# A hand-written TensorE order in the last block of a three-block kernel, with the scan's step sizes computed early

## The chip, the core and the metric

One core of a Trainium2 chip runs the whole program. The metric is the device time of one execution in microseconds (us); smaller is better. The engines are PE (TensorE), DVE (VectorE), ACT (ScalarE), POOL (GpSimd) and SP (SyncE, which issues most DMAs here). Everything is computed in 32 bits: a matrix product is made of three PE passes over a high and a low part.

## What is computed

Three blocks over 1024 tokens of 1024 features. The first is an attention with a window and a state-space mixer, the second an attention on the best 256 keys. The third, which the change is mostly about, is:

```python
h = layer_norm(x, ln_emb_g, ln_emb_b)
xs, z, bm, cm, dt_raw, glu, cgate = jnp.split(h @ w_in, SPLITS, axis=-1)
xbc = silu(causal_depthwise_conv(concat([xs, bm, cm]), ssm_conv_w, ssm_conv_b))   # 4 taps
dt = softplus(dt_raw + dt_bias)                        # step sizes
y = ssd_chunked(xh, dt, -exp(a_log), bm, cm)           # scan over 8 chunks of 128 tokens
y_ssm = group_rms((y + d_skip * xh) * silu(z)) * ssm_norm_g
u = causal_depthwise_conv(glu[..., :D] * sigmoid(glu[..., D:]), conf_conv_w, conf_conv_b)   # 31 taps
y_conf = silu(layer_norm(u, conf_ln_g, conf_ln_b)) * silu(cgate)
out = concat([y_ssm, y_conf]) @ w_out + b_out
h = layer_norm(ALPHA * h + out, ln1_g, ln1_b)
h = layer_norm(ALPHA * h + sigmoid(h @ w_ple_gate) * (p @ w_ple_proj), ln2_g, ln2_b)
```

## The kernel before, in words

A planner that simulates the program orders the instructions of every engine and chooses when a tile gets memory. It goes by the order of the trace (the order in which the Python code emits instructions), lets what is ready run first, and takes a priority: `high_priority(offset=...)` moves an instruction ahead, as for the weight loads in `wpiece` (L104). On the chip each engine runs its instructions in the order that the planner wrote.

`phase_c` (L1239) is the third block. First come the two halves of glu (L1263), with `c_vectors` (L1452) behind the first product: it loads vectors as rows and turns them with PE into columns (`cw` for the 31-tap convolution, its norm and glu's bias; `sw` for the 4-tap convolution). `xbc` (L1527) makes the raw step sizes and the 4-tap convolutions; the first tap is a DVE instruction (L1552), the other three too (L1554). The 31-tap convolution runs on DVE (L1289), 31 instructions for each of 8 tiles. `conf_norm` (L1490) takes the mean (`mu`, PE), subtracts it (L1503, DVE), squares (ACT), adds up (POOL), makes the variance (`var`, PE) and its root, spreads it (`rb`, PE), multiplies (L1523, DVE) and applies Silu (L1524).

`ssd` (L1568) begins with the step sizes: a chain of some 26 small DVE instructions on `spt`, three products (`acs`, `atot`, `acsT`), and the cumulative sums written to memory (`d_cs`). Then eight chunks follow. A chunk loads its decays as broadcast rows (`ld`, L1636), adds (L1637) and takes Exp, masks with `cb` (L1645, L1650), makes three products on POOL (`xd`, `xe`, `xh`), and for each of two groups runs `yoff`, `ydiag` (eight heads), and `inc`, which moves the state `st` on.

Beside this, PE has products that need nothing of the scan: the gate `cgate` (L1304), `z` (L1319), and the half of the output product that takes `cc` (L1348); the latter needs cc normalised and gated on POOL (L1314), and split into two parts in `msC` (L1336, L1337). They are traced after `ssd`, and the planner puts them where PE is free. Its PSUM has two banks for these, one for transposes, three (`sd`) for norm and scan, two for the convolution. Behind the block the second half of the output product (`prep`, L1368), the norm and the last gate follow.

In the second block, `DSA` (L1126) runs units of a query block and a key group: its bias loads are `lgB` (L1165), and the weights `wo` of the first half of that block's output product are loaded ahead of all units (L983).

Of the kernel before, what the change touches and what calls it, by code (L numbers as in the profile page):

```python
# [56 lines left out]
class K:  # L57
# [94 lines left out]
    def form1(self, out, hnT, tok0, wt, nk, w, wc0=0, start=True, stop=True):  # L152

        for k in range(nk):
            self.mm3(out, hnT[:, 0, k, tok0:tok0 + P], hnT[:, 1, k, tok0:tok0 + P],
                     wt[k][:, 0, wc0:wc0 + w], wt[k][:, 1, wc0:wc0 + w],
                     start and k == 0, stop and k == nk - 1)

# [676 lines left out]
def phase_b(k, x, hout, hB):  # L835
# [145 lines left out]
    with ExitStack() as c2:  # L981
        dp = c2.enter_context(k.pool("b_dsa"))
        wo = k.wchunk(Wo, 0, 512)  # L983
        ds = DSA(k, ep, dp, d_q, d_T, d_gate, kT, vB, sc, kg, mix)
        units = [(b, kv) for b in DORD for kv in range(2)]
        pipeline(ds, units, lambda b: out_tile(k, mo, gp, b, 0, [mix], wo, x, hout, "sq", 1))
# [6 lines left out]
    hnC = hp.tile([P, 2, KT, L], F32R, name="hnTC")  # L993
    gb = op.tile([P, D], F32, name="gbC")
# [131 lines left out]
class DSA:  # L1126
# [22 lines left out]
    def front(self, b, kv):  # L1149
# [10 lines left out]
        for i in range(4):  # L1160
# [3 lines left out]
            with k.tc.high_priority(offset=WPRIO):  # L1164
                nc.sync.dma_start(lg[:, :n], dap(self.d_T, h * P * 1152 + 127 + P * (7 - b), [[1151, P], [1, n]]))  # L1165
# [73 lines left out]
def phase_c(k, out, hC):  # L1239
# [8 lines left out]
    cw = vp.tile([P, 8, 36], F32, name="cw")  # L1248
# [6 lines left out]
    def stage():  # L1255
        return stg.tile([P, 512], F32, tag="s", name="stg", bufs=3)
# [21 lines left out]
    with ExitStack() as cx:  # L1278
        xbc(k, cx.enter_context(k.pool("c_xbc")), W, hnT, sw, dtt, d_xs, d_bc)
# [13 lines left out]
    conf_norm(k, up, cc, acc, cw)  # L1293
    sV.close()

    sS, (sp,) = stack(k.pool("ssd"))
    ssd(k, sp, dtt, dtx, d_xs, d_bc, d_ys, d_cs)

    for ch in range(2):
        w = k.wchunk(W, 4624 + ch * 512, 512)  # L1300
        for m in range(4):
            for th in range(2):
                ps = k.mm()
                k.form2(ps, hnT, th * 512, w, KT, m * P)  # L1304
                gt = stage()
                S.activation(gt, ps, AF.Silu)
                r0 = (ch * 4 + m) * P
                nc.scalar.dma_start(d_cg[r0:r0 + P, th * 512:th * 512 + 512], gt)
    for ct in range(8):
        for th in range(2):  # L1310
            cs = slice(th * 512, th * 512 + 512)
            cg = stg.tile([P, 512], F32, tag="cg", name="cgl", bufs=2)
            nc.sync.dma_start(cg, d_cg[ct * P:(ct + 1) * P, cs])
            G.tensor_tensor(cc[:, ct, cs], cc[:, ct, cs], cg, op=ALU.mult)  # L1314
    for ch in range(2):
        w = k.wchunk(W, 1024 + ch * 512, 512)
        for tt in range(NT):
            ps = k.mm()
            k.form1(ps, hnT, tt * P, w, KT, 512)  # L1319
            zt = stage()  # L1320
            S.activation(zt, ps, AF.Silu)
            nc.scalar.dma_start(d_z[tt * P:(tt + 1) * P, ch * 512:ch * 512 + 512], zt)
    sR.close()
    k.wdve = WDVE[4]

    with ExitStack() as co:
        op = co.enter_context(k.pool("c_o", side="right"))
        bo = op.tile([P, D], F32, name="bo")
        k.bcast_row(bo, ins["b_out_2"][0], D)
        w = [[k.wpiece(Wo, kk + 8, [(ch * 512, 512)], pool=op if ch * 8 + kk >= 13 else None, nx=3)  # L1330
              for kk in range(8)] for ch in range(2)]
        held = []
        for tt in range(NT):
# [6 lines left out]
            V.scalar_tensor_tensor(r, r, ALPHA, bo, op0=ALU.mult, op1=ALU.add)  # L1340
            held.append((tt, m, r))
            if tt == NT - 2:
                continue
            for ch in range(2):
                cs = slice(ch * 512, ch * 512 + 512)
                for t_, m, r in held:
                    ps = k.mm()
                    k.form1(ps, m, 0, w[ch], 8, 512)  # L1348
                    V.tensor_tensor(r[:, cs], ps, r[:, cs], op=ALU.add)
                    nc.sync.dma_start(d_r[t_ * P:(t_ + 1) * P, cs], r[:, cs])  # L1350
            held = []
    sS.close()
    sF.close()

# [4 lines left out]
    with ExitStack() as co:  # L1359
# [4 lines left out]
        k.bcast_row(bb, ins["ln1_b_2"][0], D)  # L1364
        w = [[k.wpiece(Wo, kk, [(ch * 512, 512)], scale=sng[:, kk:kk + 1], pool=op if ch * 8 + kk >= 13 else None, nx=3)
              for kk in range(8)] for ch in range(2)]

        def prep(tt):  # L1368
# [18 lines left out]
            r = op.tile([P, D], F32, tag="r", name="rS", bufs=2)  # L1387
            nc.sync.dma_start(r, d_r[ts_, :])
            return m, r
# [19 lines left out]
        for tt in range(NT):  # L1409
            pt = op.tile([P, 256], F32, tag="pt", name="pt", bufs=2)  # L1410
# [41 lines left out]
def c_vectors(k, p, cw, sw, dtx, sng):  # L1452
# [6 lines left out]
    rows = p.tile([36, D], F32, tag="u", name="rows", bufs=2)  # L1459
    with k.tc.high_priority(offset=2 * WPRIO):  # L1460
        nc.sync.dma_start(rows[0:31], ins["conf_conv_w_2"][0])
    for i, n in enumerate(("conf_conv_b_2", "conf_ln_g_2", "conf_ln_b_2")):
        with k.tc.high_priority(offset=2 * WPRIO):
            nc.sync.dma_start(rows[31 + i:32 + i], ins[n])
    with k.tc.high_priority(offset=2 * WPRIO):
        nc.sync.dma_start(rows[34:36], ins["b_glu_2"][0].rearrange("(a b) -> a b", a=2))
    for h in range(2):
        ps = k.tp()
        for i in range(4):
            T.transpose(ps[:, i * 36:(i + 1) * 36], rows[:, (h * 4 + i) * P:(h * 4 + i + 1) * P], k.ident[:36, :36])  # L1470
        V.tensor_copy(cw[:, h * 4:h * 4 + 4].rearrange("p a b -> p (a b)"), ps[:, :144])
# [18 lines left out]
def conf_norm(k, p, cc, acc, cw):  # L1490
# [5 lines left out]
    for th in range(2):  # L1496
        ps = k.ps("sd", "mu")
        T.matmul(ps, on, acc[:, th * 512:th * 512 + 512], start=True, stop=True)
        mu.append(ps)
    for ct in range(8):  # L1500
# [11 lines left out]
    for tt in range(NT):  # L1512
        T.matmul(ps[:, tt * 2:tt * 2 + 2], acc[:, tt * P:(tt + 1) * P], on[:, 0:2], start=True, stop=True)
    V.tensor_scalar(rs[:, 0], ps[:, :16].rearrange("p (a b) -> p a b", b=2)[:, :, 0], 1e-5, None, op0=ALU.add)
    k.rstd(rs[:, 1], rs[:, 0], 8)
    rb = [k.ps("sd", "rb0"), k.ps("sd", "rb1")]
    for tt in range(NT):
        T.matmul(rb[tt // 4][:, (tt % 4) * P:(tt % 4 + 1) * P], rs[:, 1, tt:tt + 1].to_broadcast([P, P]), k.ident,
                 start=True, stop=True)
    for ct in range(8):  # L1520
# [6 lines left out]
def xbc(k, p, W, hnT, sw, dtt, d_xs, d_bc):  # L1527
# [4 lines left out]
    for th in range(2):  # L1532
        ps = k.mm()
        k.form2(ps[:16], hnT, th * 512, w, KT, 0, 16)
        dr = p.tile([16, 512], F32, tag="dr", name="dr", bufs=1)
# [4 lines left out]
        S.activation(dtt[:, th * 4:th * 4 + 4].rearrange("p a b -> p (a b)"), ps[:, :64], AF.Copy)  # L1540
    for ci, c0 in enumerate((2048, 0, 512)):
        w = k.wchunk(W, c0, 512)
        for m in range(4):
# [8 lines left out]
            V.tensor_scalar(y, xi[:, 0:L], sw[:, ct, 0:1], sw[:, ct, 4:5], op0=ALU.mult, op1=ALU.add)  # L1552
# [5 lines left out]
            else:  # L1558
# [6 lines left out]
                nc.sync.dma_start(d_xs[:, ct * P:(ct + 1) * P].rearrange("(j p) c -> p j c", p=P), xo)  # L1565


def ssd(k, p, dtt, dtx, d_xs, d_bc, d_ys, d_cs):  # L1568
# [4 lines left out]
    t = p.tile([P, 4, P], F32, tag="ld0", name="spt", bufs=1)  # L1573
# [16 lines left out]
    ea = p.tile([P, 16], F32, name="ea")  # L1590
    S.activation(ea, dtx[:, 1], AF.Exp)
    V.tensor_scalar(ea, ea, -1.0, None, op0=ALU.mult)
    t1 = p.tile([P, 3, P], F32, tag="ld1", name="spt1", bufs=1)
    adt, one, ar = t1[:, 0].rearrange("p (a b) -> p a b", b=16), t1[:, 1], t1[:, 2]
    V.tensor_tensor(adt, dtt, ea.unsqueeze(1).to_broadcast([P, 8, 16]), op=ALU.mult)
    tri = p.tile([P, P], F32, name="tri")
# [3 lines left out]
    acs = p.tile([P, 8, 16], F32, name="acs")  # L1600
    nacs = p.tile([P, 8, 16], F32, name="nacs")
    eac = p.tile([P, 8, 16], F32, name="eac")
    dst = p.tile([P, 8, 16], F32, name="dst")
    cdc = p.tile([P, 8, 16], F32, name="cdc")
# [14 lines left out]
    nc.sync.dma_start(d_cs, ar)  # L1619
    st = [p.tile([P, 512], F32, name=f"st{g}") for g in range(2)]  # L1620
# [5 lines left out]
    for c in range(8):  # L1626
        ts_ = slice(c * P, (c + 1) * P)
        xh = p.tile([P, D], F32, tag="xh", name="xh", bufs=2)
        nc.sync.dma_start(xh, d_xs[ts_, :])
# [3 lines left out]
        for g in range(2):  # L1633
            ld = p.tile([P, 8, P], F32, tag=f"ld{g}", name="ld", bufs=1)
# [16 lines left out]
        xd = p.tile([P, D], F32, tag="xd", name="xd", bufs=1)  # L1651
        G.tensor_tensor(h3(xd), h3(xh), b64a(dtt, c), op=ALU.mult)
        xe = p.tile([P, D], F32, tag="xe", name="xe", bufs=1)
        G.tensor_tensor(h3(xe), h3(xd), b64a(dst, c), op=ALU.mult)
        G.tensor_tensor(h3(xh), h3(xh), dtx[:, 2].unsqueeze(2).to_broadcast([P, 16, 64]), op=ALU.mult)
        for g in range(2):
# [51 lines left out]
```

## Time and profile before

| | |
|---|---|
| median of 3 runs | 2106.66 us (2102.2 to 2109.16) |
| the profiled execution | 2105.1 us, its span 2103.4 us |
| PE busy | 1930.0 us (92%) |
| DVE busy | 1461.5 us (69%) |
| ACT, POOL busy | 899.0 us (43%), 920.3 us (44%) |
| mean granted PE clock | 0.962 of 2.4 GHz |

The page cuts the span into 40 slices of 52.6 us. In the third block (from about 1140 us) PE's busy share is 9 tenths or more in all slices but those from 1630 to 1735 (5 and 5) and the last (8); DVE's is 9 in most slices from 1210 to 1610. PE's clock is granted at 9 tenths or more, apart from a 6 in the slice at 1683 and an 8 beside it. The chain that ended last consists of PE's instructions for the most part.

### The profile page before, as it was taken

How to read it: one execution, taken by the hardware profiler on the slowest of the kernel's cores; microseconds unless marked ns; L12 is line 12 of the kernel's file. 1: busy time of each engine (PE TensorE's matmuls, PEld its weight loads, DVE VectorE, ACT ScalarE, POOL GpSimd, SP SyncE). 2: the span in 40 equal slices, each digit the busy share in tenths (PEclk: the TensorE clock that was granted, in tenths of full speed). 3: DMA queues.
4: the chain of work that ended last, by engine and by line, in shares of the span. 5: the costliest groups of instructions: out<-in, count | busy, mean ns of one | idle time of the engine just before them, and what ended most of it. 6: DMA issues, size and time to landing. Idle time of an engine off the chain costs nothing. (4 is left out here: it accounts for less than half of the span.)

```text
span 2103.4 us, 27623 instructions
## 1 busy us (share of the span) xinstructions
PE 1930.0 (92%) x9291; PEld 1565.0 (74%) x9291; DVE 1461.5 (69%) x2883; ACT 899.0 (43%) x1804; POOL 920.3 (44%) x774
## 2 busy tenths in 40 slices
PE   7988989989999998799988999999999559999998
PEld 6767767777888876677767788788888447778786
DVE  8465513584469988577646399999997588857737
ACT  5222326564456896677756211233322412144210
POOL 5476415545422246556457211222332576743204
PEclk9998999999999999899999999999999869999999
DMA  6543342313312212554355222223432435574442
GB/s 200 149 124 102 105 144 83 110 50 100 96 58 73 71 46 83 180 179 140 121 161 184 96 75 72 75 81 101 136 115 90 164 135 168 171 253 161 174 147 100
DMA packets 165671, 256.19 MB, mean 122 GB/s; under 512 B 29078, under 2 KB 77548, under 8 KB 165530
## 3 DMA queue, kind: packets, MB, share of 16 engines
q1 hardware_dynamic: 154026, 232.43, 34.5%
q10 hardware_dynamic: 10224, 17.82, 2.3%
q0 software_dynamic: 1280, 4.20, 0.5%
q8 instruction: 73, 1.20, 0.2%
q14 instruction: 68, 0.56, 0.1%
HBM read 185.35 MB, written 75.06 MB: 124 GB/s over the span
## 5 line engine op out<-in xcount | busy, mean ns | idle before, releaser
L123 POOL TENSOR_TENSOR w<-wraw,w 128x512 fp32r<-128x512 f32 (+1 forms) x230 | 314.8, 1384 | 657.2 <-ACT w L122 653.2
L1289 DVE SCALAR_TENSOR_TENSOR cy<-u,cw,cy 128x1024 f32<-128x1024 f32 x232 | 298.7, 1288 | 5.7
L122 ACT ACTIVATE w<-wraw 128x512 fp32r<-128x512 f32 (+1 forms) x230 | 141.2, 623 | 190.6 <-DMA wraw<-in_w_in_dram 54.7
L149 PE MATMUL mm<-hnTC,w 128*128 128x512 f32 (+1 forms) x336 | 131.6, 392 | 0.0
L150 PE MATMUL mm<-hnTC,w 128*128 128x512 f32 (+1 forms) x336 | 131.5, 391 | 0.0
L148 PE MATMUL mm<-hnTC,w 128*128 128x512 f32 (+1 forms) x336 | 131.5, 391 | 0.0
L150 PE MATMUL mm<-w,ms 128*128 128x512 f32 x256 | 106.0, 414 | 10.0 <-POOL ms L1022 8.5
L1167 POOL TENSOR_TENSOR lgB<-lgB,sc 128x1024 f32<-128x1024 f32 (+5 forms) x48 | 80.7, 1711 | 72.9 <-DMA lgB<-d_T 53.5
L148 PE MATMUL mm<-w,ms 128*128 128x512 f32 x256 | 104.9, 410 | 8.2 <-ACT ms L1021 8.1
L1078 ACT ACTIVATE tkj<-sc,tks 128x896 bf16<-128x896 f32 (+2 forms) x93 | 96.6, 1041 | 22.3 <-DVE tks L1074 19.5
L149 PE MATMUL mm<-w,ms 128*128 128x512 f32 x256 | 103.2, 403 | 0.0
L148 PE MATMUL mm<-w,hnTB 128*128 128x512 f32 x192 | 77.3, 404 | 11.9 <-ACT qo L401 8.9
L148 PE MATMUL mm<-w,hnTA 128*128 128x512 f32 (+1 forms) x192 | 73.3, 385 | 9.2 <-DVE qo L415 9.2
L148 PE MATMUL mm<-hnTB,w 128*128 128x512 f32 (+2 forms) x208 | 78.4, 377 | 0.3 <-ACT hnTB L172 0.3
L149 PE MATMUL mm<-hnTB,w 128*128 128x512 f32 (+2 forms) x208 | 78.1, 376 | 0.0
L150 PE MATMUL mm<-hnTB,w 128*128 128x512 f32 (+2 forms) x208 | 78.1, 375 | 0.0
L150 PE MATMUL mm<-w,hnTB 128*128 128x512 f32 x192 | 75.9, 396 | 0.0
L149 PE MATMUL mm<-w,hnTB 128*128 128x512 f32 x192 | 75.3, 395 | 0.0
L150 PE MATMUL mm<-w,hnTA 128*128 128x512 f32 (+1 forms) x192 | 73.4, 383 | 0.0
L149 PE MATMUL mm<-w,hnTA 128*128 128x512 f32 (+1 forms) x192 | 73.2, 382 | 0.0
L148 PEld LDWEIGHTS mm<-hnTC,w 128*128 128x128 f32 (+1 forms) x336 | 61.6, 183 | 14.5
L149 PEld LDWEIGHTS mm<-hnTC,w 128*128 128x128 f32 (+1 forms) x336 | 61.6, 183 | 14.4
(611 smaller groups left out, 5883.1 us busy)
## 6 DMA issues: line engine op xcount, KB each, us to landing
wraw<-in_w_in_dram SPq DMA_DIRECT2D x56, 256.0 KB
wraw<-in_od_w_in_dram SPq DMA_DIRECT2D x48, 256.0 KB
wraw<-in_ev_w_in_dram SPq DMA_DIRECT2D x32, 256.0 KB
wraw<-in_w_in_dram SPq DMA_DIRECT2D x64, 128.0 KB
wraw<-in_w_out_dram SPq DMA_DIRECT2D x32, 256.0 KB
ld<-d_cs SPq DMA_DIRECT2D x16, 512.0 KB
hr<-h SPq DMA_DIRECT2D x24, 256.0 KB
d_T<-d_row SPq DMA_DIRECT2D x8, 576.0 KB
```

Of the source, the lines that this page charges most:

```text
L122: nc.scalar.activation(t[:, 0, :o], raw[:, :o], AF.Copy)
L123: nc.gpsimd.tensor_tensor(t[:, 1, :o], raw[:, :o], t[:, 0, :o].bitcast(F32), op=ALU.subtract)
L148: mm(out, aH, bH, start=start, stop=False)
L149: mm(out, aH, bL, start=False, stop=False)
L150: self.last = mm(out, aL, bH, start=False, stop=stop)
L1078: S.activation(self.junk(n), sc[b], AF.Sign, bias=cand[:, i:i + 1], accum_out=cnt[:, i:i + 1])
L1167: G.tensor_tensor(lg[:, :n], lg[:, :n], self.masks[b], op=ALU.add)
L1289: V.scalar_tensor_tensor(py if i < 30 else y, u[:, i:i + L], cw[:, ct, i:i + 1], py, op0=ALU.mult, op1=ALU.add)
```

## The change

- `steps1`, `steps2`: the products of `form1` and `form2` as generators that stop after each of the eight steps (three matmuls).
- In `phase_c`, gate, z and the output half that takes cc stand in one generator, `filling`: 128 steps each. A block `manual_schedule` on PE keeps PE's order as traced. In it, `take(n)` emits n steps: 186 first, 43, 8 and 0 at three stops of `conf_norm`, and 0, 4, 3 at stops of `ssd`, five in a chunk; the rest follow. The gate products on POOL are traced at the first four stops of `ssd`.
- The step sizes leave `ssd` for `ssd_steps`, which `xbc` calls after the raw step sizes.
- xbc's first tap is an ACT instruction.
- The rows for `cw` are loaded and turned in `phase_b`'s last loop.
- `wo` is loaded behind the bias loads of the second unit of `DSA`.
- Scan tiles: `xh`, `xd`, `xe` in halves, three `ld` in one tag, `y`, `xe`, `xd` declared first. `b_out` is added on POOL in the next stage. The output half's weights are all split on ACT and POOL.

```diff
@@ phase_b
-        wo = k.wchunk(Wo, 0, 512)
+        def front_first(b, kv):
+            front(b, kv)
+            if (b, kv) == units[1]:
+                with tc.issue_after(ds.bias_load.ins):
+                    wo.extend(k.wchunk(Wo, 0, 512))
...
+        if tt == 1:
+            for h in range(2):
+                ps = k.tp()
+                for i in range(4):
+                    T.transpose(ps[:, i * 36:(i + 1) * 36], rows[:, (h * 4 + i) * P:(h * 4 + i + 1) * P], k.ident[:36, :36])
+                V.tensor_copy(k.cw[:, h * 4:h * 4 + 4].rearrange("p a b -> p (a b)"), ps[:, :144])
@@ phase_c
-    def stage():
-        return stg.tile([P, 512], F32, tag="s", name="stg", bufs=3)
+    def stage(name="stg"):
+        return stg.tile([P, 512], F32, tag="s", name=name, bufs=4)
...
+    with tc.manual_schedule(engines={mybir.EngineType.PE}):
+        take(128 + 58)
+        norm = conf_norm(k, up, cc, acc, cw)
+        for n in (43, 8, 0):
+            next(norm)
+            take(n)
+        next(norm, None)
+        sV.close()
+        sS, (sp,) = stack(k.pool("ssd"))
+        gated = 0
+        for i, _ in enumerate(ssd(k, sp, steps, dtt, dtx, d_xs, d_bc, d_ys, d_cs)):
+            for _ in range(min(4, 16 - gated)):
+                ct, cs = gated % 8, slice(gated // 8 * 512, gated // 8 * 512 + 512)
+                cg = stage("cgl")
+                nc.sync.dma_start(cg, d_cg[ct * P:(ct + 1) * P, cs])
+                G.tensor_tensor(cc[:, ct, cs], cc[:, ct, cs], cg, op=ALU.mult)
+                gated += 1
+            take(0 if i == 0 else 4 if i < 5 else 0 if i < 7 else 3)
+        take(500)
...
-            V.scalar_tensor_tensor(r, r, ALPHA, bo, op0=ALU.mult, op1=ALU.add)
...
-                    V.tensor_tensor(r[:, cs], ps, r[:, cs], op=ALU.add)
+                    V.scalar_tensor_tensor(r[:, cs], r[:, cs], ALPHA, ps, op0=ALU.mult, op1=ALU.add)
...
             nc.sync.dma_start(r, d_r[ts_, :])
+            G.tensor_tensor(r, r, bo, op=ALU.add)
@@ xbc
+    steps = ssd_steps(k, p, vp, dtt, dtx, d_cs)
...
-            V.tensor_scalar(y, xi[:, 0:L], sw[:, ct, 0:1], sw[:, ct, 4:5], op0=ALU.mult, op1=ALU.add)
+            S.activation(y, xi[:, 0:L], AF.Identity, scale=sw[:, ct, 0:1], bias=sw[:, ct, 4:5])
@@ ssd
+        for g in range(2):
+            xd = half("xd", "xd")
+            G.tensor_tensor(h3(xd), h3(xhs[g]), b64(dtt, g, c), op=ALU.mult)
+            xds.append(xd)
+        for g in range(2 if c < 7 else 0):
+            xe = half("xe", "xe")
+            G.tensor_tensor(h3(xe), h3(xds[g]), b64(dst, g, c), op=ALU.mult)
+            xes.append(xe)
...
             T.matmul(po, bct[:, 2 + g], st[g], start=True, stop=True)
...
+            yield
             pd = k.ps("sd", "ydiag")
```

## Rows read from the trace of the kernel before

**Rows 1.** Busy time of each engine in stretches; after the instructions PEclk, DMA share, GB/s.
```profile
1650.00:1696.00 46.00, 10.22 (x59) 8.96 (x58) 38.21 (x64) 17.78 (x20) 24.22 (x17) 0.64 0.60 205
1696.00:1720.00 24.00, 14.69 (x52) 10.24 (x51) 15.66 (x16) 6.13 (x9) 21.20 (x13) 0.55 0.43 147
...
1740.00:1760.00 20.00, 15.65 (x57) 10.86 (x57) 18.55 (x15) 3.45 (x4) 13.86 (x6) 0.83 0.48 139
1760.00:1830.00 70.00, 70.00 (x356) 55.04 (x356) 62.54 (x58) 14.04 (x16) 53.66 (x23) 1.00 0.53 175
1830.00:1876.00 46.00, 41.21 (x198) 32.90 (x196) 25.52 (x32) 12.59 (x22) 20.28 (x12) 0.96 0.70 237
1876.00:2104.00 228.00, 215.43 (x998) 176.63 (x998) 145.08 (x244) 58.88 (x114) 64.92 (x52) 0.98 0.43 153
```

**Rows 2.** Waits of PE from 1380 us on: total us, times, longest.
```profile
PE acs L1606 <- DVE spt L1595: 35.8, 1, 35.8
PE ydiag L1664 <- DVE ld L1650: 12.1, 2, 9.3
```

**Rows 3.** Timeline of DVE around the norm: start, duration, what, idle before.
```profile
1602.93 1.22 DVE L1292 TENSOR_TENSOR acc<-acc,cc 128x1024 f32<-128x1024 f32 x1
...
1617.33 9.64 DVE L1503 TENSOR_TENSOR cc<-cc,mu 128x512 f32<-128x512 f32 x16
...
1660.58 9.64 DVE L1523 TENSOR_TENSOR cc<-cc,rb 128x512 f32<-128x512 f32 x16
```

**Rows 4.** Timeline of PE at the norm's last products.
```profile
1657.37 1.95 PE L1518 MATMUL rb<-ident,rsc 128*128 128x128 f32 x16
```

**Rows 5.** Timeline of ACT, one of the z tiles taken out of PSUM.
```profile
1583.25 0.60 ACT L1321 ACTIVATE stg<-mm 128x512 f32<-128x512 f32 x1 [4.84 <-PE mm L150]
```

**Rows 6.** The chain that ended last, one chunk of the scan: start, us, what.
```profile
1806.68 1.73 PE ydiag L1664 x16
1808.41 0.92 PE inc L1671 x2
```

**Rows 7.** Timeline of DVE: xbc's last tile, the last step-size instruction.
```profile
1479.70 1.39 DVE L1552 TENSOR_SCALAR xy<-xi,sw 128x1024 f32<-128x1024 f32 x1 [2.48 <-ACT xi L1550]
...
1488.09 1.27 DVE L1554 SCALAR_TENSOR_TENSOR xy<-xi,sw,xy 128x1024 f32<-128x1024 f32 x1
...
1694.66 0.29 DVE L1595 TENSOR_TENSOR spt<-dtt,ea 128x128 f32<-128x128 f32 x1
```

**Rows 8.** Groups of DVE, 1150 to 1660: busy, mean ns, idle before.
```profile
L1552 DVE TENSOR_SCALAR xy<-xi,sw 128x1024 f32<-128x1024 f32 x12 | 10.9, 907 | 5.7 <-ACT xi L1550 5.5
```

**Rows 9.** Stretches, as rows 1: the turned vectors, the second block's first units.
```profile
1155.00:1170.00 15.00, 10.71 (x49) 8.38 (x48) 3.85 (x12) 3.88 (x5) 2.45 (x2) 0.66 0.27 97
860.00:890.00 30.00, 17.10 (x85) 14.34 (x85) 10.85 (x55) 21.39 (x74) 15.55 (x19) 0.72 0.74 224
```

**Rows 10.** Timeline of PE behind the turned vectors.
```profile
1163.73 0.79 PE L148 MATMUL pb<-hnTC,w 128*128 128x512 f32 x1 [2.48 <-ACT stg L1275]
```

**Rows 11.** Timeline of all engines in the second block's first units.
```profile
866.57 2.97 SPq L110 DMA_DIRECT2D wraw<-in_od_w_out_dram  x2
...
872.15 0.29 DVE L1174 CUSTOM_DVE_ANT_0 lgB<-s,lgB 128x128 f32<-128x128 f32 x1 [9.66 <-DMA lgB<-d_T]
```

**Rows 12.** Groups of POOL, 1600 to 1880.
```profile
L1314 POOL TENSOR_TENSOR cc<-cc,cgl 128x512 f32<-128x512 f32 x16 | 25.3, 1594 | 11.1 <-DMA cgl<-d_cg 9.8 <-ACT cc L1524 1.3
...
L1337 POOL TENSOR_TENSOR msC<-cc,msC 128x1024 fp32r<-128x1024 f32 x8 | 21.5, 2690 | 11.4 <-ACT msC L1336 11.4
```

**Rows 13.** Timeline of ACT: a table load and the instruction behind it.
```profile
1668.15 1.28 ACT L1524 ACT_TABLE_LOAD   x1
1669.44 9.17 ACT L1524 ACTIVATE cc<-cc,cw 128x1024 f32<-128x1024 f32 x8
```

**Rows 14.** Waits of all engines, 1600 to 1880: the scan's broadcast loads.
```profile
DVE ld L1637 <- DMA ld<-d_cs: 17.0, 11, 3.5
```

**Rows 15.** Groups of DVE, 1600 to 1880.
```profile
L1637 DVE CUSTOM_DVE_ANT_1 ld<-ld,nacs 128x1024 f32<-128x1024 f32 x16 | 27.9, 1749 | 17.0 <-DMA ld<-d_cs 17.0
```

More of the change, by code (lines that the diff above doesn't have):

```diff
@@ L157, in form1, with steps1, steps2 @@
                      start and k == 0, stop and k == nk - 1)
+    def steps1(self, out, hnT, tok0, wt, nk, w):
+        for k in range(nk):
+            self.mm3(out, hnT[:, 0, k, tok0:tok0 + P], hnT[:, 1, k, tok0:tok0 + P],
+                     wt[k][:, 0, :w], wt[k][:, 1, :w], k == 0, k == nk - 1)
+            yield
+    def steps2(self, out, hnT, tok0, wt, nk, m0):
+        for k in range(nk):
+            self.mm3(out, wt[k][:, 0, m0:m0 + P], wt[k][:, 1, m0:m0 + P],
+                     hnT[:, 0, k, tok0:tok0 + 512], hnT[:, 1, k, tok0:tok0 + 512], k == 0, k == nk - 1)
+            yield
     def form2(self, out, hnT, tok0, wt, nk, m0, m=P):
@@ L1278, in phase_c @@
     with ExitStack() as cx:
-        xbc(k, cx.enter_context(k.pool("c_xbc")), W, hnT, sw, dtt, d_xs, d_bc)
+        steps = xbc(k, cx.enter_context(k.pool("c_xbc")), vp, W, hnT, sw, dtt, dtx, d_xs, d_bc, d_cs)
     for ct in range(8):
@@ L1309, in phase_c @@
[L1309 to L1329, printed above, removed]
+    held = ExitStack()
+    def filling():
+        for ch in range(2):
+            w = k.wchunk(W, 4624 + ch * 512, 512)
+            for m in range(4):
+                for th in range(2):
+                    ps = k.mm()
+                    yield from k.steps2(ps, hnT, th * 512, w, KT, m * P)
+                    gt = stage()
+                    S.activation(gt, ps, AF.Silu)
+                    r0 = (ch * 4 + m) * P
+                    nc.scalar.dma_start(d_cg[r0:r0 + P, th * 512:th * 512 + 512], gt)
+        for ch in range(2):
+            w = k.wchunk(W, 1024 + ch * 512, 512)
+            for tt in range(NT):
+                ps = k.mm()
+                yield from k.steps1(ps, hnT, tt * P, w, KT, 512)
+                zt = stage()
+                S.activation(zt, ps, AF.Silu)
+                nc.scalar.dma_start(d_z[tt * P:(tt + 1) * P, ch * 512:ch * 512 + 512], zt)
+        sR.close()
+        op = held.enter_context(k.pool("c_o", side="right"))
@@ L1345, in phase_c, with take @@
                 cs = slice(ch * 512, ch * 512 + 512)
-                for t_, m, r in held:
+                for t_, m, r in late:
                     ps = k.mm()
-                    k.form1(ps, m, 0, w[ch], 8, 512)
-                    V.tensor_tensor(r[:, cs], ps, r[:, cs], op=ALU.add)
+                    yield from k.steps1(ps, m, 0, w[ch], 8, 512)
+                    V.scalar_tensor_tensor(r[:, cs], r[:, cs], ALPHA, ps, op0=ALU.mult, op1=ALU.add)
                     nc.sync.dma_start(d_r[t_ * P:(t_ + 1) * P, cs], r[:, cs])
-            held = []
+            late = []
+    fill = filling()
+    def take(n):
+        for _ in range(n):
+            next(fill, None)
+    with tc.manual_schedule(engines={mybir.EngineType.PE}):
[17 more added lines that the diff above has]
+        take(500)
+    held.close()
     sS.close()
     sF.close()
+    k.wdve = WDVE[4]
     k.psum(mm=4, tp=2, th=2)
@@ L1458, in c_vectors @@
             k.bcast_row(dtx[:, i], ins[n][0], 16)
[L1459 to L1471, printed above, removed]
     ps = k.tp()
@@ L1524, in conf_norm, with xbc @@
         S.activation(cc[:, ct], cc[:, ct], AF.Silu, bias=cw[:, ct, 33:34], scale=cw[:, ct, 32:33])
-def xbc(k, p, W, hnT, sw, dtt, d_xs, d_bc):
+def xbc(k, p, vp, W, hnT, sw, dtt, dtx, d_xs, d_bc, d_cs):
     nc = k.nc
@@ L1599, in ssd @@
     V.memset(one, 1.0)
[L1600 to L1604, printed above, removed]
+    nacs = vp.tile([P, 8, 16], F32, name="nacs")
+    eac = vp.tile([P, 8, 16], F32, name="eac")
+    dst = vp.tile([P, 8, 16], F32, name="dst")
+    cdc = vp.tile([P, 8, 16], F32, name="cdc")
     ps = k.ps("sd", "acs")
@@ L1619, in ssd, with half @@
     nc.sync.dma_start(d_cs, ar)
+    return tri, nacs, eac, dst, cdc
+def ssd(k, p, steps, dtt, dtx, d_xs, d_bc, d_ys, d_cs):
+    nc, ins = k.nc, k.ins
+    V, S, G, T = nc.vector, nc.scalar, nc.gpsimd, nc.tensor
+    f = lambda a: a.rearrange("p a b -> p (a b)")
+    tri, nacs, eac, dst, cdc = steps
+    first = {t: [p.tile([P, 512], F32, tag=t, name=n, bufs=2) for _ in range(2)]
+             for t, n in (("y", "yS"), ("xe", "xe"), ("xd", "xd"))}
+    def half(tag, name):
+        return first[tag].pop(0) if first[tag] else p.tile([P, 512], F32, tag=tag, name=name, bufs=2)
     st = [p.tile([P, 512], F32, name=f"st{g}") for g in range(2)]
```

84 lines of the change are left out of this document (46 added, 38 removed).

## The prediction

> **What bounds the kernel now.** I began with the page's slices: PE is 92% busy, and two of the 40 slices stand out at 5, both near 1660 to 1710 us. So the time is PE's work plus PE's holes, and I cut the last block into windows by what PE does [rows 1]. PE is full until 1650. From 1650 to 1696 it is busy 10.22 of 46 us, from 1696 to 1720 14.69 of 24, from 1740 to 1760 15.65 of 20 and from 1830 to 1876 41.21 of 46: 35.8 + 9.3 + 4.4 + 4.8 = 54.2 us of holes. The granted clock falls with them: over 1696 to 1720 it is 0.55, so the 14.69 busy us ran nearly all at 1.2 GHz and would have taken about 6 less; the same reading gives about 2.5 for 1740 to 1760 (0.83) and 1.8 for 1830 to 1876 (0.96). Holes and low clock are together 54.2 + 10.3 = 64.5 us.
>
> The waits of PE then say why [rows 2]: one of 35.8 us, acs for spt (the first step-size matmul for the chain of small vector instructions before it), and ydiag for ld, 12.1 us in two waits. The order on DVE says what came before [rows 3]: the 31-tap convolution ends at 1604.15, the subtraction of the mean starts only at 1617.33, and the multiplication by the deviation runs 1660.58 to 1670.2. PE did its rb matmuls at 1657.37 [rows 4] and then had nothing: gates and z were used up, and the output half needs the normalised cc, the scan needs its step sizes. After 1876 PE is busy 215.43 of 228, so the end is set by PE in order, and a hole closed in the last block reaches the end.
>
> **The change, part by part.**
>
> *Fill kept for the holes.* One fill step (three matmuls) costs 0.68 us: two z tiles of eight steps finish 5.44 us apart [rows 5]. There are 128 steps of gate, 128 of z and 128 of output. Before, z was spent when rb ran. Now 128 + 58 stand ahead of the mean's matmuls, 43 and 8 inside the norm, so 147 steps (100 us) are left for the scan, 115 of them inside it. The work is the same; only its place moves. The scan's own PE work per chunk, from the chain, is 2 x (1.73 ydiag + 0.92 inc + yoff, of inc's form, taken as 0.9) plus about 0.5 for cb, 7.5 us [rows 6]; with 15 steps of fill a chunk is 17.7 us of PE. That such a mixture runs without a hole is shown: from 1760 to 1830 PE is busy 70 of 70 us at clock 1.00 while DVE is busy 62.54 and POOL 53.66 [rows 1]. So the steady part should be PE-bound.
>
> *Step sizes early.* The 35.8 us wait goes. About 26 DVE instructions of some 0.29 us (the last of them stands in [rows 7]), 7.5 us, move into the convolution stretch, where DVE is the fuller engine. Against them the first of four taps of 12 tiles goes to ACT: 10.9 us off DVE [rows 8]. DVE ends the convolution about 3 us earlier, near 1601; 72 z steps stood ahead of the mean before (the rest, by 0.68 us, ran from 1617 to 1657), so with 58 PE now asks for it near 1606 and does not wait. Cost taken: 0; bounds -3 to +8 (all of the 7.5 late, no help from the taps).
>
> *Vectors turned in the second layer.* From 1155 to 1170 PE is busy 10.71 of 15 us at clock 0.66, ending in a wait of 2.48 us of pb for ACT, whose bias vector is one of those being turned [rows 9, 10]. Idle 4.3 and about 3.5 lost to the clock; the eight small transposes (1 us) move to a stretch where PE is busy anyway, and the other vectors stay. I take 6 gained; bounds 0 and 8.
>
> *Output weights of layer two behind the second unit's bias loads.* From 860 to 890 PE is busy 17.10 of 30 us [rows 9]. The SP queue issued two weight loads at 866.57 and the second unit's bias loads behind them, and DVE waited 9.66 us for these, until 872.15 [rows 11]. They can now go some 10 us earlier. But ACT only then comes to the first unit's exponential, and eight weight pieces fall into a stretch that already moves 224 GB/s. I take 2 gained; bounds -10 (the wait comes back for the third unit, behind eight weight loads) and +10 (all of it goes).
>
> *Scan tiles in halves, output bias to a later stage.* Eight DVE additions of D columns leave the scan; eight POOL additions of as many enter the following stage, where POOL is busy 64.92 of 228 us and PE hides them [rows 1]: cost 0; without that cover a late addition delays the residual's sum by one POOL instruction of that size, 2.7 us as msC's [rows 12], eight times: 21, which I hold for excluded since each has a tile's time of about 20 us. The weight pieces that DVE split in the scan go to POOL; this is in (c) below.
>
> *What is late next.* Three waits replace the large one. (a) All 16 multiplications by the deviation (9.6 us [rows 3]) must be done before the first yoff, since the scan's PSUM banks are three and two hold the deviation: PE has only cb to do meanwhile, 9 us. (b) Chunk 1 has 9 fill steps, 13.7 us of PE, against DVE's 62.54 us for the 3.8 chunks of 18.4 us (7.5 + 16 x 0.68) between 1760 and 1830, 16.4 each [rows 1]: 3 us. (c) The first output matmul needs msC(0), whose tile lies where hnT was until z's last step: ACT about 1.0, then POOL 2.69, and POOL has by then 16 gates of 1.59 (25 us), the weight pieces and two chunks' products [rows 12]: 8 us, between 4 (POOL free) and 20 (all gates ahead). Each hole of this size lowers the clock to 1.2 GHz; after ydiag's hole of 9.3 us PE ran some 8 us of what was left of 1696 to 1720 at that level, 4 us lost. Two or three such drops: 8 us. Together 28 us, bounds 10 and 50.
>
> ACT alternates between Silu (z's tiles) and Exp (the scan) in (b); the trace has a table load at 1.28 us, the next instruction starting 0.01 us behind it [rows 13], and two of them are inside the 3 us. The Trainium skill, ScalarE: Activation LUTs, "What ACT_TABLE_LOAD costs", puts a switch at about 2.66 us with a drain behind the load. By that the sum would be about 3 us higher; the row decides.
>
> **Sum.** The profiled execution is 2105.1 us (span 2103.4 and 1.7 around it), 1.6 under the median of 2106.66, so it can stand for it. 2105.1 - 64.5 + 28 - 6 - 2 = 2060.6. I forecast 2060.
>
> **Rivals.**
> *A: the holes come back at the scan's start.* (c) at 20, (a) followed by a wait of the first ydiag, and PE held up ahead of the fill by xbc's last transposes if the hand order lets no gate step pass them: the last tap of xbc ends at 1489.4, and its input was there at 1479.7 [rows 7], so 10 us and a clock drop of 4. 28 becomes 28 + 12 + 14 = 54: 2086. For it: POOL was already busy 21.20 of 24 us from 1696 to 1720 [rows 1] with less to do. Against: the z steps between (a) and (c) give POOL time.
> *B: slower. The fixed order blocks at every half chunk.* Where a planner's order put output matmuls in front of a late ydiag, now the fill traced behind it waits. Mechanism: L1650 sits on DVE behind the next chunk's L1637, which waits for its broadcast load. Price per hit: 3.5 (the longest such wait) + 1.75 (L1637 itself) and 2 of clock, about 7 us [rows 14, 15]. From seven of the 14 later half chunks on the whole gain of 45 is spent; with eight the time is 2116. Against: 1760 to 1830 shows DVE 11% free. The Trainium skill, PSUM — Partial Sum Buffer, "Engine vs sequencer instructions", says that matmuls start and complete in program order; by that rule each blocked one holds all behind it, and the trace agrees at ydiag's 9.3 us wait, in which no other matmul ran.
> *C: everything hides.* Residue 10, 860 to 890 halved: 2105.1 - 64.5 + 10 - 8 - 8 = 2035. Against: (a) has no cover in the hand order.
> *D: it does not do what it says* (loads or tiles wait for memory as before, so that spt comes no earlier): within 5 us of 2105. Against: d_cs then needs nothing but the convolved vectors.
>
> **How the numbers follow.** Forecast 0.64 (own range 2044 to 2076), A 0.17, C 0.08, B 0.07, D 0.04. Range 2034 to 2090: it takes C's and A's times and leaves out B, D and the tails. About 0.3%, 6 us, is what a measurement of this kernel tells from no change. Faster 0.88, same 0.04, slower 0.08.
>
> **What would show it.** Right: no wait of acs over 5 us; PE's holes from the mean to the end of the output half near 20 us in sum, the largest at the first yoff; clock 1.00 from chunk 2 on; the following stage starting near 1830 rather than 1876; the pb wait gone. Wrong: ydiag waits at many half chunks (B), POOL ahead of the first msC by more than 10 us or a hole ahead of the first gate steps (A), or a stage after the scan that lengthens.

## The result, and the profile after

The changed kernel takes 2078.20 us (median of 4 runs, 2076.27 to 2082.0) against 2106.11 beside it: 0.987 of the kernel before, 95% interval 0.9856 to 0.9884. A repeat on another chip gave 0.9877 (0.9862 to 0.9891). The forecast was 2060 (2034 to 2090): the direction and the range held, but of the 46 us forecast only 28 came. Below, "after" is the changed kernel; times of different runs are compared by their ratio to the kernel before on the same chip, whose median went from 2101.67 to 2111.45 from chip to chip. 0.001 is 2.1 us.

The profiled execution of after is 2079.29 us, its span 2077.6. First the page's busy times, then the stretches of the last block (columns as in [rows 1]; the first two lines answer to [rows 9], the others to [rows 1]).

```profile
PE 1939.3 (93%) x9291; PEld 1569.5 (76%) x9291; DVE 1408.7 (68%) x2847; ACT 922.2 (44%) x1831; POOL 946.9 (46%) x812
```

```profile
860.00:890.00 30.00, 22.66 (x105) 17.81 (x106) 14.21 (x64) 24.36 (x73) 15.93 (x14) 0.77 1.00 293
1150.00:1160.00 10.00, 8.19 (x26) 6.32 (x26) 1.40 (x5) 1.75 (x2) 0.00 (x0) 0.66 0.15 57
1640.00:1670.00 30.00, 19.63 (x62) 14.42 (x63) 24.91 (x26) 17.89 (x17) 30.00 (x22) 0.66 0.62 207
1670.00:1700.00 30.00, 21.02 (x90) 15.71 (x89) 13.51 (x14) 14.69 (x18) 30.00 (x20) 0.83 0.64 209
1700.00:1760.00 60.00, 58.46 (x284) 44.84 (x284) 41.56 (x43) 10.31 (x15) 44.62 (x33) 0.97 0.59 186
1760.00:1800.00 40.00, 36.57 (x162) 27.82 (x162) 24.67 (x29) 6.79 (x8) 22.88 (x17) 0.91 0.50 159
```

PE before was busy 1930.0 us with the same 9291 instructions. It is now busy 9.3 us longer: nothing was added, so that is time at the lower clock (1640 to 1670 stands at 0.66, and 1760 to 1800 at 0.91, where before it was full at 1.00). The clock records of the two traces bear it out: 105.7 us of PE's busy time fall into stretches that were granted 1.2 GHz, the lower of its two levels, against 88.0 before, and half of the difference is 8.9 us. The waits of PE from 1590 to 1870 (total us, times, longest) say what took the place of acs [rows 2]:

```profile
PE ydiag L1734 <- DVE ld L1711: 12.0, 6, 4.1
PE yoff L1728 <- DVE st L1681: 5.2, 1, 5.2
PE mm L150 <- POOL msC L1359: 3.9, 1, 3.9
PE cb L1703 <- DMA bct<-d_bc: 3.4, 1, 3.4
PE tph L195 <- DVE smS L1432: 2.7, 1, 2.7
PE mm L148 <- ACT msC L1358: 2.1, 1, 2.1
PE var L1554 <- POOL acc L1550: 0.3, 1, 0.3
```

acs is gone; twelve waits in seven rows, the longest of 5.2 us, make 29.6 us, where there were 54.2 us of holes.

Where the 25.8 us of span (2103.4 to 2077.6) come from, by four landmarks in both traces: up to the second block's last transpose of its scores 8.2 us (1066.9 before, 1058.7 after); from there to the first long tap 1.6 (127.3, 125.7); the long convolution, from that tap to the end of its last sum, 3.5 (410.0, 406.5); from there to the first square of the stage behind the scan 15.1 (261.2, 246.1); the rest -2.5 (238.1, 240.6). PE is busy without a break in the long convolution in both traces (410.0 of 410.0 us, 406.5 of 406.5), so the 3.5 us there are work that is left for the stretch behind it. The two together gave 18.6 where 36.5 was forecast, and 9.8 came ahead of them, where 8 was forecast. A single trace is good to a few us only: runs with the same order of instructions up to the first landmark reach it between 1055.2 us (e9) and 1062.9 (e7).

One mechanism that the prediction had not named is on SP. Timelines of SP, POOL and DVE of after:

```profile
1616.51 19.00 SPq L1394 DMA_DIRECT2D cgl<-d_cg  x4
1635.56 0.90 SPq L1690 DMA_DIRECT2D xh<-d_xs  x2
1636.50 0.43 SPq L1692 DMA_DIRECT2D bct<-d_bc  x1
1637.05 0.91 SPq L1697 DMA_DIRECT2D ld<-d_cs  x2
```

```profile
1639.48 2.04 POOL L1716 TENSOR_TENSOR xd<-xh,dtt 128x512 f32<-128x512 f32 x2 [7.25 <-DMA xh<-d_xs]
```

```profile
1636.86 9.65 DVE L1566 TENSOR_TENSOR cc<-cc,rb 128x512 f32<-128x512 f32 x16 [6.37 <-PE rb L1560]
1646.57 1.03 DVE L1681 MEMSET st<- 128x512 f32 x2
1647.51 1.55 DVE L1698 CUSTOM_DVE_ANT_1 ld<-ld,nacs 128x1024 f32<-128x1024 f32 x1
```

The gate loads share their tiles with the z evictions, so four of them stand on SP for 19 us until z tiles are stored, and chunk 0's loads stand behind them. On DVE the sixteen products by the deviation come first, then the zeroing of the state, then chunk 0's sums; PE's first yoff starts when the zeroing ends (1647.2), ydiag at 1657.55.

### The profile page after: what moved, and what is told of

It reads as the page before. It is cut to its first block, busy times and chain, and to the rows that moved or that the text cites. A ratio compares the mean times of both kernels' runs of the same rounds, so it can differ in the third digit from the quotient of the medians.

```text
span 2077.6 us, 27679 instructions
## 1 busy us (share of the span) xinstructions
PE 1939.3 (93%) x9291; PEld 1569.5 (76%) x9291; DVE 1408.7 (68%) x2847; ACT 922.2 (44%) x1831; POOL 946.9 (46%) x812
## 4 chain that ended last, share of the span: by engine, by line
PE 59%; DVE 15%; DMA 9%; issue 6%; ACT 5%; POOL 5%; SPq 1%; DVEq 0%; POOLq 0%; ACTq 0%
PE mm L150 11%; PE mm L148 11%; PE mm L149 11%; DVE tkj L1114 2%; PE ydiag L1734 1%; PE pb L148 1%; PE pb L150 1%; PE pg L148 1%; PE pg L150 1%; PE pb L149 1%; PE pg L149 1%; PE pa L149 1%; PE pa L150 1%; PE pa L148 1%; POOL w L123 1%
## 5 line engine op out<-in xcount | busy, mean ns | idle before, releaser
L123 POOL TENSOR_TENSOR w<-wraw,w 128x512 fp32r<-128x512 f32 (+1 forms) x238 | 326.3, 1385 | 653.8 <-ACT w L122 647.2
L122 ACT ACTIVATE w<-wraw 128x512 fp32r<-128x512 f32 (+1 forms) x238 | 145.9, 623 | 186.2 <-DMA wraw<-in_w_in_dram 47.2
```

What stands on the lines that cost most here:

```text
L122: nc.scalar.activation(t[:, 0, :o], raw[:, :o], AF.Copy)
L123: nc.gpsimd.tensor_tensor(t[:, 1, :o], raw[:, :o], t[:, 0, :o].bitcast(F32), op=ALU.subtract)
```

## The experiments

**e1, gate loads in tiles of their own.**

```diff
-        return stg.tile([P, 512], F32, tag="s", name=name, bufs=4)
+        return stg.tile([P, 512], F32, tag="s", name=name, bufs=2)
-                cg = stage("cgl")
+                cg = stg.tile([P, 512], F32, tag="cg", name="cgl", bufs=2)
```

> The kernel after, but the gate loads (cgl) have two tiles of their own and the evictions' stage has two instead of four, so that no gate load waits for a z tile to be stored. Theory 'queue': SP takes its DMAs in order, and the four gate loads that wait 1616 to 1635 us for z's stores hold back chunk 0's xh, bct and ld; with them gone from the front these loads go out about 5 us earlier, the wait of cb for bct (3.4 us) goes, and the time falls by 3 to 6 us against the kernel after (2072 to 2075). Rival 'vector work': chunk 0 waits in any case for VectorE's sixteen deviation products (to 1646.6 us); then the wait of cb goes, the one of yoff grows by as much, and the time stays within 2 us of 2078. Rival 'stage': two stage tiles are too few for the evictions, and the time rises by 3 us or more.

0.9862 (0.9842 to 0.9881): not to be told from after. From the end of the convolution, cb came 3.8 us earlier (46.4 us instead of 50.2) but the first ydiag only 1.6 (65.0, 66.6). The queue on SP is real and nearly free: the wait moved on to DVE. The first rival was right.

**e2, the second block's output weights loaded first again.**

```diff
-        wo = []
+        wo = k.wchunk(Wo, 0, 512)
...
-        ds.front = front_first
```

> The kernel after, with the second block's output weights again loaded before the first attention unit, as in the kernel before. Prediction's term: 2 us slower than the kernel after (bounds -10 to +10). Reading of the two traces: the attention phase's first transposes came 9 us earlier in the kernel after, with nothing else changed ahead of them, so 8 to 10 us slower (2086 to 2088).

0.9889 (0.9874 to 0.9904), about 3 us slower than after. The stretch 860 to 890 is back to what it was in [rows 9], with the wait on DVE:

```profile
PE s L148 <- DVE stB L1207: 9.6, 1, 9.6
```

```profile
860.00:890.00 30.00, 17.30 (x86) 14.61 (x85) 10.79 (x55) 21.57 (x74) 16.76 (x20) 0.72 0.72 218
```

By the trace the attention phase ends 5 to 9 us later than in e1, e3 and e4 on the same chip (1068.5 against 1062.1, 1063.8 and 1059.3). The time shows less than that; the prediction's 2 was nearer than my reading of 8 to 10.

**e3, the conformer's vectors turned in the last block again.**

```diff
-    cw = k.cw
+    cw = vp.tile([P, 8, 36], F32, name="cw")
...
+    rows = p.tile([36, D], F32, tag="u", name="rows", bufs=2)      # in c_vectors, as before
```

> The kernel after, with the conformer's vectors loaded and turned again at the head of the last block, as in the kernel before. Prediction's term: 6 us slower than the kernel after (0 to 8). Reading of the two traces: the shift between them grows by 2 to 3 us over the first gated-unit tiles, and ScalarE's wait there is still in the trace, so 1 to 3 us slower (2079 to 2081).

0.9907 (0.9892 to 0.9921), 7 us slower than after: the prediction's 6, not the 1 to 3 that the two traces suggested. PE's wait there:

```profile
PE tp L1511 <- DMA rows<-in_conf_ln_b_dram: 8.5, 1, 8.5
```

SP's order gives the reason. In the kernel before, the vectors' rows went out ahead of the weights:

```profile
1142.98 0.35 SPq L1464 DMA_DIRECT2D rows<-in_conf_ln_b_dram  x1
...
1147.59 0.35 SPq L110 DMA_DIRECT2D wraw<-in_w_in_dram  x1
```

In e3 they stand behind eight weight loads, though nothing of that step differs from the kernel before:

```profile
1146.56 7.87 SPq L110 DMA_DIRECT2D wraw<-in_w_in_dram  x8
1155.22 0.29 SPq L1502 DMA_DIRECT2D rows<-in_conf_conv_w_dram  x1
```

So the move is worth 1.6 us against the place the rows had before (1.4 to 3.3 by the other runs that keep the move, whose stretch takes 124.0 to 125.9 us), and 7 against the place that the planner gives them now. Why it puts them there no run shows.

**e4, TensorE's order left to the planner.**

```diff
-    with tc.manual_schedule(engines={mybir.EngineType.PE}):
+    with ExitStack():
```

> The kernel after with TensorE's order left to the planner: the same work traced in the same order, the step sizes early, the split tiles, but nothing fixed by hand. Theory 'early steps do it': the wait of 35.8 us at the step sizes goes by itself, and the time stays within 4 us of the kernel after (2074 to 2082). Theory 'order does it': the planner again spends the z and gate products ahead of the conformer's norm and of the scan, 10 to 25 us are lost in 1620 to 1760 us, and the time is 2088 to 2103.

0.9834 (0.9821 to 0.9847): faster than after by 8 to 9 us. The hand order is not where the gain is; it costs. The two longest waits of PE:

```profile
PE ydiag L1734 <- DVE ld L1711: 8.9, 1, 8.9
PE yoff L1728 <- DVE st L1681: 8.9, 1, 8.9
```

Both stand at the start of the scan, and none of the five later ones for ld is left. But all of PE's waits together make 29.2 us, as many as in after (29.6): they are fewer and longer. What is less is the clock's part: from 1590 to 1870 us, 25.1 us of PE's busy time are at 1.2 GHz, in after 35.8 and in its repeat e5 31.5. The planner puts the mean's product 11.3 us behind the end of the last sum instead of 5.9, but it needs 164.7 us from the first ydiag to the following stage's first square, where the hand order needs 179.5. From the convolution's end to the end of the program the profiled execution is only 3.8 us shorter (482.9, 486.7), so the sign of the cost is surer than its size.

**e5, after once more.** 

> The kernel after, unchanged, beside the three others on one chip, so that differences of a few us can be read without the step from chip to chip: 0.987 of the kernel before (0.985 to 0.989) by every theory.

0.9877 (0.9862 to 0.9891), and PE busy 1935.4 us with nearly the same waits (31.6 us of holes from 1590 to 1870): of the 9.3 us by which PE's busy time rose, 4 vary from run to run.

**e6, e4 without the zero state of chunk 0.**

```diff
+            if c:
                 T.matmul(po, bct[:, 2 + g], st[g], start=True, stop=True)
                 V.tensor_tensor(h3(y), h3(po), b64(eac, g, c), op=ALU.mult)
...
+                if c:
                     V.tensor_tensor(h3(st[g]), h3(st[g]), b64(cdc, g, c), op=ALU.mult)
                     V.tensor_tensor(st[g], pi, st[g], op=ALU.add)
+                else:
+                    V.tensor_copy(st[g], pi)
```

> The kernel of e4 (TensorE ordered by the planner), and chunk 0 of the scan without its zero state: no product with st, no scaling of it, no memset; the sums are those of the reference. In e4 the first yoff waits 8.9 us for the memset that stands behind the sixteen deviation products on VectorE, and ydiag another 8.9 us for ld. Prediction's term (a), that the first yoff's wait is a cost by itself: about 9 us faster than e4 (0.979 of the kernel before). Rival, that VectorE's products set the start of the scan and the wait only moves from yoff to ydiag: within 3 us of e4 (0.982 to 0.985).

0.983 (0.9815 to 0.9845), as e4. The yoff wait is gone and has moved:

```profile
PE ydiag L1733 <- DVE ld L1709: 27.5, 3, 18.2
```

The longest is 18.2 us, about the two 8.9 of e4 together, and PE's idle time from the convolution's end on stays the same (43.8 us in e4, 43.0 here). Term (a) of the prediction was no cost of its own: what PE waits for at the scan's start is DVE's chain (sixteen products, sums, then exponentials and products), whichever product asks first.

**e7, e4 with the step sizes at the head of the scan again.**

```diff
-    steps = ssd_steps(k, p, vp, dtt, dtx, d_cs)      # in xbc
-    tri, nacs, eac, dst, cdc = steps
+    tri, nacs, eac, dst, cdc = ssd_steps(k, p, steps, dtt, dtx, d_cs)
```

> The kernel of e4 with the step sizes, their sums along the chunk and the exponentials computed at the head of the scan again, as in the kernel before, all else as in e4. Theory 'early steps': the chain from softplus to the sums stands behind the deviation products on VectorE once more, TensorE waits for it, 15 to 25 us slower than e4 (0.990 to 0.995 of the kernel before). Rival 'gates and stages': the gain came from the gates' and the z products' place and the split tiles, and the planner fills the wait: within 5 us of e4.

0.9919 (0.9903 to 0.9934), 18 us slower than e4. The old wait is back in two pieces: a z product that waits for ScalarE, which has gone over to the norm's Silu, and acs.

```profile
1665.12 0.80 PE L148 MATMUL mm<-w,hnTC 128*128 128x512 f32 x1 [17.00 <-ACT stg L1348]
1680.07 0.77 PE L1651 MATMUL acs<-spt,tri 128*128 128x128 f32 x2 [6.87 <-DVE spt L1641]
```

A third wait, new and not explained by any run, stands at the first transposes of the following stage (3.1 us in e4):

```profile
PE tph L195 <- ACT yO L1436: 13.0, 1, 13.0
```

From the convolution's end to the first square it takes 259.2 us, e4 238.3. The early step sizes carry half of e4's gain of 35 us: without them e7 is still 17 us faster than the kernel before.

**e8, the step sizes early and nothing else, in the kernel before.**

```diff
+    steps = ssd_steps(k, p, vp, dtt, dtx, d_cs)
     for ci, c0 in enumerate((2048, 0, 512)):
```

> The kernel before with one part of the change alone: the step sizes, their sums and exponentials computed in the stage of the short convolution, before its channels. Theory 'early steps': the wait of 35.8 us goes, some of it comes back at the first yoff and ydiag (as 17.8 us of waits in e4), 15 to 20 us faster than the kernel before (0.990 to 0.993). Rival 'gates and stages': the wait comes back whole, since the loop's filling work stands elsewhere in the trace order: within 5 us of the kernel before.

1.0092 (1.0074 to 1.011): 19 us slower, which neither theory allowed. By the landmarks 6.8 us are lost ahead of the convolution (127.3, 134.1), 8.0 in it (410.0, 418.0) and 6.2 behind it (261.2, 267.4). The first is SP's order as in e3:

```profile
1148.31 8.62 SPq L110 DMA_DIRECT2D wraw<-in_w_in_dram  x8
1157.71 0.29 SPq L1461 DMA_DIRECT2D rows<-in_conf_conv_w_dram  x1
```

The second is DVE, busy 249.30 of 260 us from 1330 to 1590 and so with little room: the chain of step sizes lengthens the stage, and the tap is not moved. PE, never idle there before, now waits 5.3 us: 3.5 at xbc's transposes and 1.8 at acsT. The third: acs waits no more, but PE has no filling work for the first chunks. The last z product starts at 1675.0 us and the first of the output half only at 1752.3; in e4 they follow on each other (1681.6, 1685.0). The stretches from 1670 to 1760:

```profile
1670.00:1700.00 30.00, 9.93 (x45) 7.10 (x43) 28.21 (x34) 15.77 (x18) 19.71 (x12) 0.64 0.78 275
1700.00:1760.00 60.00, 41.84 (x155) 28.31 (x154) 50.89 (x46) 9.39 (x11) 51.96 (x27) 0.67 0.54 184
```

The scan runs bare, with DVE busy 50.89 of 60 us and POOL 51.96, at a clock of 0.67. So the step sizes early are worth 18 us with the rest of the change around them (e4 against e7) and nothing alone. e8 lacks every other part of the change at once, so which part it misses, the filling work or the room on DVE, is argued here and not shown.

**e9, by hand up to the norm, planner from the scan on** (the with-block ends ahead of these lines).

```diff
-        sV.close()
-        sS, (sp,) = stack(k.pool("ssd"))
+    sV.close()
+    sS, (sp,) = stack(k.pool("ssd"))
```

> The kernel after with TensorE's order by hand only up to the end of the conformer's norm, and left to the planner from the scan on. In e4 (planner throughout) the means' product came 12.5 us after the last tap's sum instead of 6.0, and the scan from the first ydiag to the third block of products took 15 us less than in the kernel after. Theory 'hand order helps at the norm and hurts in the scan': the early mean is kept and the scan is the planner's, 4 to 7 us faster than e4 (0.980 to 0.9815 of the kernel before). Rival 'VectorE sets the start': the six us come back as a wait at the first yoff and ydiag, within 2 us of e4 (0.9825 to 0.9845). Rival 'the norm is no place of its own': as slow as the kernel after (0.987).

0.9825 (0.9812 to 0.9837): 10 us faster than after and 2 under e4, which lies inside both intervals. So the hand order's cost, 10 us by the times and 6.6 by the profiled executions from the convolution's end on (480.1, 486.7), lies inside the scan. At the norm it gives 2 or nothing, since the first ydiag then waits for ld all the same (the 12.5 us of the expectation count from the last sum's start, the 6.0 from its end; from its end they are 11.3 and 5.9):

```profile
PE ydiag L1734 <- DVE ld L1711: 10.1, 3, 9.2
```

**e10, e9 and e6 together.** 

> e9 with chunk 0 of the scan freed of its zero state (the edit of e6), the sums those of the reference. Theory: as e6 beside e4, the wait moves from yoff to ydiag and only the two products and the memsets go: 0 to 4 us faster than e9 (0.978 to 0.981 of the kernel before, if e9 gives 0.980 to 0.9815). Rival, that with the mean early VectorE is no longer late at the scan's start and the wait at yoff goes by itself: 5 us or more faster than e9.

0.9811 (0.9798 to 0.9823), 3 us under e9, as by the theory, though the two intervals do not part them; the ydiag wait is 13.7 us in 3.

**e11, the short convolution's first tap on VectorE again.**

```diff
-            S.activation(y, xi[:, 0:L], AF.Identity, scale=sw[:, ct, 0:1], bias=sw[:, ct, 4:5])
+            V.tensor_scalar(y, xi[:, 0:L], sw[:, ct, 0:1], sw[:, ct, 4:5], op0=ALU.mult, op1=ALU.add)
```

> The kernel after with the short convolution's first tap on VectorE again (12 instructions), as in the kernel before. Prediction's term: step sizes and taps together cost nothing. Reading of the traces: VectorE is busy 97% from the first long tap on, the long convolution took 410 us in the kernel before, 406.5 in the kernel after, 402.8 in e7 (taps moved, no step sizes) and 418 in e8 (step sizes, taps not moved); so the tap's move gave 11 us there and the step sizes cost 4 to 8; with the tap back the conv's end is 8 to 12 us later and the time 6 to 12 us more (0.990 to 0.993 of the kernel before). Rival 'cover': filling work on TensorE hides it, within 2 us of the kernel after.

0.9916 (0.9901 to 0.9931), 9 us slower than after. The last sum over the taps starts at 1600.5 instead of 1589.7, of which 1.5 were there at the first tap:

```profile
L1326 DVE TENSOR_TENSOR acc<-acc,cc x6: 1216/1224/1525, 1325.7 to 1600.5; 128x1024 f32<-128x1024 f32 x6
```

DVE's length is not all of it. PE, never idle in the convolution in after, now waits there as in e8, and 6.6 us of its busy time are at 1.2 GHz:

```profile
PE tp L1607 <- ACT xy L1599: 3.3, 1, 3.3
PE acsT L1663 <- DVE spt L1653: 1.8, 1, 1.8
```

**e12, e10 with e1's tiles and chunk 0's sums ahead of the sixteen products.**

```diff
-        next(norm, None)
...
+        if i == 0:
+            with tc.issue_after(k.add.ins):       # the last sum ld+nacs of chunk 0
+                next(norm, None)
```

> e10 with two more edits: the gate loads have tiles of their own (the edit of e1), and the sixteen deviation products are issued behind the two sums ld+nacs of chunk 0 on VectorE, which stood behind them. In e10 ydiag waits 13.7 us in 3 for ld, whose chain (sums 3.1 us, exponentials, products 4.4 us) begins when the deviation products end. Theory 'VectorE's order sets the scan's start': with the gate loads off SP's front ld lands while VectorE is idle before the deviation products, the sums and exponentials go beside them, ydiag's first wait falls from 9.9 to about 5 us, 3 to 6 us faster than e10 (0.978 to 0.980 of the kernel before). Rival 'POOL sets it': the gates and xd on POOL, busy without a break from 1640 us, take the wait over at xd and msC, within 2 us of e10 (0.980 to 0.982). Rival 'two stage tiles are too few': slower than e10.

0.9808 (0.9784 to 0.9832), 2064.05 us: with e10 the fastest, not to be told from it, and some 14 us faster than after. The sums did go early (1631.44 us, before the products at 1635.41), and the first ydiag waits no more. Two other waits take its place:

```profile
1658.97 2.05 PE L1745 MATMUL inc<-xe,bt 128*128 128x512 f32 x2 [6.93 <-POOL w L123]
1678.14 3.65 PE L1735 MATMUL ydiag<-xd,ld 128*128 128x64 f32 x16 [9.26 <-DVE ld L1711]
```

The trace puts the first down to a weight piece on POOL, but inc does not read it, and xe was ready at 1636.2 us. What inc reads and what came last is bt, which ACT copied only then, behind six Silu instructions and six weight pieces. The second goes back to a load of chunk 1, which DVE's sum waits for, with the mask and the products behind it:

```profile
1658.51 0.36 ACT L1709 ACTIVATE bt<-cb 128x256 f32<-128x256 f32 x1
...
1673.50 1.36 DVE L1698 CUSTOM_DVE_ANT_1 ld<-ld,nacs 128x1024 f32<-128x1024 f32 x1 [6.63 <-DMA ld<-d_cs]
```

PE is idle 24.2 us from 1580 to 1860, in e10 23.9. The theory was right that the start moves, the rival that the time does not; but the waits went to ACT's order and to a load, not to POOL.

## Why the prediction was right in direction and short in size

- *Step sizes early: the 35.8 us wait goes.* Right, and shown twice: acs waits no more in after, and e7 loses 18 us without it.
- *What is late next, 28 us.* This is the step that failed: it measured about 47. The holes were put at 20 and are 29.6 (31.6 in e5). (a), 9 at the first yoff, came as 3.4 at cb, 5.2 at yoff and 4.1 at ydiag, 12.7, one wait on DVE's order (e6). (b), 3 at chunk 1, came as five later ydiag waits of 7.9 in all. (c), 8 at msC(0), came as 6.0. The following stage's first transposes added 2.7. The clock was put at 8, for two or three drops. There were six, and half of PE's busy time at 1.2 GHz from 1590 to 1870 is 17.9 us (15.8 in e5); before it was 11.5, from 1590 to 1880, with three. So twelve small waits cost more clock here than eight waits of 54.5 us did before, and more than the eight waits of 29.2 us in e4 (12.5). The sign of a clock at 1.00 from chunk 2 on did not come: it is 0.91 from 1760 to 1800.
- *The order by hand.* The sum credited the filled holes to early step sizes and fill together. e4 and e9 part them: the fixed order of the fill is not needed and costs 8 to 10 us by the times. That fill must stand ready among the half chunks is argued from e8 and not shown apart. The cost is rival B in small: the fill traced behind a late ydiag waits with it. An example on DVE:

```profile
1676.85 1.55 DVE L1698 CUSTOM_DVE_ANT_1 ld<-ld,nacs 128x1024 f32<-128x1024 f32 x1 [2.66 <-DMA ld<-d_cs]
1678.33 0.41 DVE L1706 TENSOR_TENSOR cb<-cb,tri 128x256 f32<-128x256 f32 x1
1678.84 3.98 DVE L1711 TENSOR_TENSOR ld<-ld,cb 128x1024 f32<-128x1024 f32 x2
```

```profile
1680.76 1.97 PE L1734 MATMUL ydiag<-xd,ld 128*128 128x64 f32 x16 [3.00 <-DVE ld L1711]
```

  The products (L1711) stand behind the sum, the sum behind its load, and PE stands 3.0 us. B gave 7 us for each hit and asked for seven; there were five of 1.6 us on average. As e4 has no less waiting in all, what they cost against it is by these traces mostly their clock.
- *Step sizes and taps cost nothing.* Right as a sum, wrong in its parts, and it had no business being zero: DVE is busy 95% of the convolution (390.5 of 410.0 us; [rows 8] gave the 10.9 us of taps). The taps gave 9 (e11). The step sizes lengthen the convolution by 4 to 8 (402.8 us in e7 to 407.0 in e4; 410.0 before to 418.0 in e8). With both it is 3.5 shorter.
- *Vectors turned in the second layer, 6.* e3 gives 7, yet only 1.6 against the trace of before: pb's wait for ACT stayed, 2.7 us after 2.48 [rows 10].
- *Output bias in the next stage, 0.* That stage takes 2.5 us longer (238.1, 240.6; 241.2 in e5). No run takes the addition out, so what of it is the bias's stays open.
- *Output weights of layer two, 2.* 3 by e2's time, 5 to 9 by its trace, where that landmark spreads over 7.7 from run to run: the 9.66 us wait of [rows 11] went, and a wait of 5.2 us for qTB came.
- *Rival A, holes back at the scan's start.* Nearly this, but not by its mechanism: the short convolution's transposes held nothing up in after (PE is busy 410 of 410 us from 1180 to 1590), though they do in e8 and e11, and 2086 was 8 too high. C and D are out.
- The Trainium skill, ScalarE: Activation LUTs, "What ACT_TABLE_LOAD costs", puts a switch near 2.66 us, a drain behind the load included. Seven switches between 1651 and 1694 us took 1.28 us each in the trace of after, and behind six of them ACT's next instruction starts within 0.02 us (1667.61 + 1.28 to 1668.90). So the measured row holds, as the prediction took it; no run here isolates what the switches cost PE.

Left open: which of the later ydiag waits the clock loss hangs on. No run changed the clock alone. PE's 24 us of holes in e10 and e12 remain, and no run moved bt ahead on ACT, or chunk 1's loads ahead on SP, to see whether they end there.

## What to carry to other kernels

Price the wait that goes and the filling work that must stand in its place apart: an early chain alone made this kernel 19 us slower, 6 of them in the scan where no filling work stood ready, and the same filling work under a fixed order gave 8 to 10 us of the gain back. Where another engine nearly fills a stage (DVE in the convolution), look at what is moved in or out of it although PE bounds the kernel: 10.9 us of taps cost 9 us here. And where a first wait is taken away, follow the chain of its releaser to the end (products, sums, exponentials, copies, loads), and test a releaser that the profile names against what the instruction reads: e1, e6 and e12 each removed a wait and got it back one step on.

## What the runs showed that was not expected

- The clock's loss can grow while the holes shrink: after has 24.6 us fewer holes in the last block (54.2 to 29.6), and PE's same instructions took 5 to 9 us longer in two profiles of it. The mean granted clock hides this: it rose from 0.962 to 0.965, since less of the time at 1.2 GHz was idle.
- An edit in one stage can move a transfer in another: eight weight loads ahead of the vectors' rows cost 7 us in e3 and e8, where the code of that step had not changed.
